# A hybrid attention, RWKV-7 and Hyena layer in fp32 on one core: the wkv output and its group norm with time on partitions, and two interleaved orders of small matrix products

## The chip, the cores and the metric

The kernel runs on one core of one Trainium2 chip. The metric is the device time of one execution in microseconds (us). The core has a matrix engine (TensorE, PE in the profile; PEld is its weight load), a vector engine (VectorE, DVE), a scalar engine (ScalarE, ACT), GpSimd (POOL) and a queue engine (SP) that issues most DMAs. A difference under about 0.2% (6 us) can't be told from no change here.

## What is computed

The reference is one step of a diffusion backbone with one layer. 128 context tokens and 256 latent tokens go through it together, so nearly every matrix product has 384 columns.

```python
h = rms_norm(x, ln1) * (1 + sc1) + sh1
proj = h @ w_in                       # attention q/k/v | wkv r/k/v | Hyena x0/x1/v | 3 gates
merged = g_a * (o_a @ w_pa) + g_r * (o_r @ w_pr) + g_c * (o_c @ w_pc)
x = x + ga1 * (merged @ w_out)
x = x + ga2 * (square(relu(h2 @ w_ff1 + b_ff1)) @ w_ff2 + b_ff2)
# the wkv mixer, 16 heads of 64, forward and backward in time, state S (value x key):
S = S * w_t + (S @ -kk_t) b_t^T + v_t k_t^T ;   y_t = S @ r_t
y = y_forward + flip(y_backward)
yn = (y - mean(y)) * rsqrt(var(y) + GN_EPS)     # per time step and head: the group norm
o_r = (yn * gn_g + gn_b + bonus) * g
```

## The kernel before

**Big products.** Each big product is made in tiles of 128 output features by 384 tokens. An fp32 weight block is split by ACT into a rounded part `whi` (L217) and by DVE into the rest `wlo` (L233), and each of the 16 blocks of 128 input features takes three matmuls (`hh·whi`, `hh·wlo`, `hl·whi`). They are the rows with `main` in the first part of the program, here called big matmuls.

**The mixers are side work.** While the big matmuls of the input projection run (about 235 to 1245 us in the profile), generators for the three mixers hand in small fp32 products between them: `rwkv(j)`, `hyena(j)`, `attention(j)`, for j = 0 to 7, each for two heads (128 features). After every third big matmul `side_step` advances each generator whose inputs should be there by a model of the three engines' clocks (`clk`), if DVE and ACT are not too far ahead of PE in that model. So the order on each engine is fixed when the program is built, by modelled costs, and each engine executes its list in order. Where a mixer of the next j needs a buffer of the last one, `drain` advances the generators alone, with no big matmuls between, until that mixer is done (in `a_done`, for instance, until attention j-1 is marked).

**The wkv mixer** works in 6 chunks of 64 time steps: two of the context (segment 0), four of the latents (segment 1), each in both directions d. First, 32x32 blocks of a triangular matrix are inverted on DVE and with small products: `quads` are the four blocks (two directions by two halves), each on its own 32 rows and columns of PE; `q1` is the first block of each direction in time (partitions 0 to 31 and 96 to 127). The products `g<-Z,Q` (48 for each j) and `g<-Q,Z` (24) go to two PSUM banks `g2[:, 0]` and `g2[:, 1]`. Then four stages `st` go along the chunks; a stage has two chunks (one for each direction) for each live segment, so 4, 4, 2 and 2. In each stage the output y of a chunk is made with features on partitions: one 128x128-weight product with the state (`misc<-kr,SZ`), and two with 64 weight columns (`misc<-Gm,UV`), one for each head. ACT copies them to `ys`.

**The tail** adds the directions, takes head means with a product by a block matrix (`misc<-ys,cst` 128x384), squares, sums them to time rows (`head_sums`, six products of 2 columns), takes the inverse root, turns that back (`spread`, three transposes), scales, and multiplies by the gate (`misc<-lg,l`).

**Attention** makes its output in three blocks of 128 queries; the two heads are in the two halves of the columns (`misc<-aPT,vt`), first all key tiles of head 0, then those of head 1.

Of the kernel before, what the change touches and what calls it, by code (L numbers as in the profile page):

```python
# [23 lines left out]
NT = NP + NS  # L24
# [110 lines left out]
def kernel(ctx: ExitStack, tc: tile.TileContext, t: dict, o: dict):  # L135
# [79 lines left out]
    def acopy(out, in_):  # L215
        spend("act", (free(in_) / 1.2 + 93) / 1000.0, out, (in_,))
        scalar.copy(out, in_)  # L217
# [20 lines left out]
    def add(out, a, b):  # L238
        tt(out, a, b, ALU.add)
# [15 lines left out]
    def turn(out, in_):  # L255
        dve(out, (in_,))
        vector.transpose(out, in_)  # L257
# [20 lines left out]
    def C(name):  # L278
        a, n = COFF[name]
        return cst[:, a:a + n]  # L280
# [425 lines left out]
    def open_a():  # L706
        p = pa.enter_context(tc.tile_pool(name="pa", bufs=1))

        def T(name, shape, dt=F32):
            P[name] = p.tile(shape, dt, name=name)  # L710
            return P[name]

        T("rkv", [128, 2, NT])
        T("v", [128, NT + 64])
        T("TW", [128, 2, NT]); T("TA", [128, 2, NT])
        T("cum", [128, NT]); T("tx", [128, NT])
        T("Pe", [128, 6, 65]); T("PC", [128, 2, 6])
        T("kk", [128, NT])
        for d in range(2):
            T(f"kr{d}", [128, 6, 2, 64]); T(f"bk{d}", [128, 6, 2, 64])  # L720
            T(f"UV{d}", [128, 6, 128]); T(f"Gm{d}", [128, 6, 2, 128])
        T("Z", [128, 32, 32]); T("L", [128, 32, 32]); T("Z2", [128, 32, 32])
        T("X", [128, 12, 64]); T("Q32", [128, 12, 32])
        T("SZ", [128, 2, 2, 128]); T("ys", [128, 2, NT])
        T("hy", [128, 3, NT]); T("qk", [128, NT]); T("kc", [128, 512]); T("va", [128, NT])
        P["pool"] = p
        flat = P["Z2"].rearrange("p i j -> p (i j)")
        P["QT"] = flat[:, :384].rearrange("p (b i) -> p b i", i=32)
        P["tmp"] = flat[:, 512:624]
        P["W0"] = P["L"].rearrange("p i j -> p (i j)")[:, 512:768].rearrange("p (a b) -> p a b", a=2)  # L730
        scalar.dma_start(out=T("dfi", [97, 1280]), in_=t["dfti"])
        nc.gpsimd.memset(P["Z"], 0.0)
        nc.gpsimd.memset(P["X"], 0.0)
        vcopy(P["Q32"], C("eye").unsqueeze(1).to_broadcast([128, 12, 32]))
# [34 lines left out]
    def take_g2():  # L769
        yield from take("g2")  # L770
# [4 lines left out]
    def take_m():  # L775
        i = yield from take(0, 1)
        return i
# [79 lines left out]
    def rwkv(j):  # L857
        rk_, v = P["rkv"], P["v"]
        r, k = rk_[:, 0], rk_[:, 1]
        TW, TA, cum, tx, Pe, PC = (P[n] for n in ("TW", "TA", "cum", "tx", "Pe", "PC"))  # L860
        kk = P["kk"]
        kr, bk, UV, Gm = ([P[f"{n}{d}"] for d in range(2)] for n in ("kr", "bk", "UV", "Gm"))
        Z, L, Z2, X, QT, tmp, W0, SZ, ys, Q32 = (P[n] for n in ("Z", "L", "Z2", "X", "QT", "tmp", "W0", "SZ", "ys", "Q32"))
        bon = P["pool"].tile([128, NT], F32, tag="bon", name="bon", bufs=2)
        l2 = P["pool"].tile([128, 3, 128], F32, tag="l2", name="l2", bufs=2)
        cj = slice(j * 128, j * 128 + 128)
# [79 lines left out]
                yield  # L946
        turn(Z, L.rearrange("p i j -> p j i"))
        turn(Z2, L)
        yield from take_g2()
        yield  # L950

# [9 lines left out]
                C("eye")[rows[d], x].unsqueeze(1).to_broadcast([64, 12, 16]), ALU.mult, ALU.add)  # L961
        yield
        for b in range(12):
            for d, q, s in quads:
                mm(g2[s, 0, b * 32:b * 32 + 32], Q32[s, b], DD[d][s, :, b])
        for b in range(12):
            for d in range(2):
                s = q1[d]
                mm(g2[s, 1, b * 32:b * 32 + 32], DD[d][s, :, b], Q32[s, b])
        yield  # L970
        for d, q, s in quads:
            (acopy if d else vcopy)(X[s, :, 32 * q:32 * q + 32], g2[s, 0, :NT].rearrange("p (b t) -> p b t", t=32))
# [23 lines left out]
        for st in range(4):  # L996
            live = [(sg, d, seqs[sg][d][st]) for sg in ((1, 0) if st < 2 else (1,)) for d in range(2)]
            for sg in ((1, 0) if st < 2 else (1,)):
                first = sg == 0 and st == 0
                if not first:  # L1000
                    for d in range(2):
                        mm(PQ[d][rows[d], sg * 128:sg * 128 + 128], kr[d][:, seqs[sg][d][st], 0], SZ[:, sg, d], stop=False)
                for h in range(2):
                    for d in range(2):
                        c = seqs[sg][d][st]
                        mm(PQ[d][rows[d], sg * 128 + 64 * h:sg * 128 + 64 * h + 64], Gm[d][rows[1 - d], c, h, 0:64],
                           UV[d][rows[1 - d], c, 64 * h:64 * h + 64], start=first, stop=first or h == 1)
            yield
            n = 256 if st < 2 else 128
            s0 = 0 if st < 2 else 128  # L1010
            acopy(W0[rows[0]].rearrange("p a b -> p (a b)")[:, s0:s0 + n], PQ[0][rows[0], s0:s0 + n])
            vcopy(W0[rows[1]].rearrange("p a b -> p (a b)")[:, s0:s0 + n], PQ[1][rows[1], s0:s0 + n])
            yield
            for sg in ((1, 0) if st < 2 else (1,)):
                for h in range(2):
                    for d in range(2):
                        c = seqs[sg][d][st]
                        mm(PQ[1 - d][rows[d], sg * 128 + 64 * h:sg * 128 + 64 * h + 64], X[rows[d], 2 * c + h],
                           W0[rows[d], sg, 64 * h:64 * h + 64])
            yield  # L1020
            for sg, d, c in live:
                cpy = acopy if d == 0 else vcopy
                cpy(UV[d][rows[d], c], PQ[1 - d][rows[d], sg * 128:sg * 128 + 128])
            yield
            for sg, d, c in live:
                if sg == 1 and st == 3:
                    continue
                mm(PQ[d][:, 256 + sg * 128:384 + sg * 128], bk[d][:, c].rearrange("p a x -> p (a x)"), UV[d][:, c])
            m = yield from take_m()
            for n, (sg, d, c) in enumerate(live):  # L1030
                y = M[m][:, n * 64:n * 64 + 64]
                first = sg == 0 and st == 0
                if not first:
                    mm(y, SZ[:, sg, d], kr[d][:, c, 1], stop=False)
                for h in range(2):
                    mm(y[64 * h:64 * h + 64], UV[d][:, c, 64 * h:64 * h + 64], Gm[d][:, c, h, 64:128],
                       start=first, stop=True)
            yield
            for sg, d, c in live:
                if sg == 1 and st == 3:  # L1040
                    continue
                ps, S = PQ[d][:, 256 + sg * 128:384 + sg * 128], SZ[:, sg, d]
                if sg == 0 and st == 0:
                    stt(S, ps, PC[:, d, c:c + 1], C("bones"), ALU.mult, ALU.mult)
                else:
                    add(S, ps, S)
                    stt(S, S, PC[:, d, c:c + 1], C("bones"), ALU.mult, ALU.mult)
            for n, (sg, d, c) in enumerate(live):
                acopy(ys[:, d, c * 64:c * 64 + 64], M[m][:, n * 64:n * 64 + 64])
            give(m)  # L1050
            if st == 1:
                for d in range(2):
                    pool_q.dma_start(out=o["state"][d, j], in_=SZ[:, 0, d])
            if st == 3:
                mark("chain", j)
            yield
        y, yc2 = ys[:, 0], ys[:, 1]
        add(y, ys[:, 0], ys[:, 1])
        m = yield from take_m()
        yield  # L1060
        mm(M[m][:, :NT], C("bones"), y)
        yield
        stt(y, M[m][:, :NT], -1.0 / 64, y, ALU.mult, ALU.add)
        dep()
        act(yc2, y, AF.Square)
        yield
        head_sums(M[m], yc2)
        yield
        rs = rsqrt(M[m][:, 0:6], 6, 1.0 / 64, 64e-5)
        dep()  # L1070
        acopy(ch(yc2), rs.unsqueeze(2).to_broadcast([128, 6, 64]))
        yield
        spread(M[m], yc2)
        yield
        mul(y, y, M[m][:, :NT])
        dep()
        act(y, y, AF.Identity, bias=V("gn_b", j), scale=V("gn_g", j))
        yield
        mm(M[m][:, :NT], l2[:, 2], P["lg"])
        yield  # L1080
        add(y, y, bon)
        mul(y, y, M[m][:, :NT])
        give(m)
        pool_q.dma_start(out=Osp[1, cj], in_=y)
        mark("tail", j)

# [55 lines left out]
    def attention(j):  # L1142
# [31 lines left out]
        for blk in range(3):  # L1174
# [42 lines left out]
            yield  # L1217
            m = yield from take_m()
            kts = (0,) if blk == 0 else (1, 2, 3)
            for h in range(2):  # L1220
                for i, kt in enumerate(kts):
                    mm(M[m][64 * h:64 * h + 64, 0:128], vt[:, kt, 64 * h:64 * h + 64], PT[:, h, i],
                       start=(i == 0), stop=(i == nk - 1))
            yield
# [473 lines left out]
```

## Time and profile before

| | |
|---|---|
| median of 3 runs | 2991.66 us (2987.81 to 2993.28) |
| the profiled execution | 2992.65 us, its span 2990.9 us |
| PE busy | 2937.0 us (98%), 20845 matmuls |
| DVE busy | 1864.9 us (62%) |
| ACT busy | 1226.1 us (41%) |
| DMA | 452.02 MB, mean 151 GB/s |

A matmul's busy time is modelled and overlaps its neighbours, so a sum of busy times is not the time that PE gave to something. The time that a group of small products takes is read from starts: from the start of the first to the start of the next big matmul. An fp32 product that is no transpose shows as two rows (x2); a big matmul and a transpose show as one. The start of one big matmul follows another's by 0.17 us.

### The profile page before, as it was taken

The page shows a single profiled execution, that of the slowest core. Times are in us where ns is not written, and L with a number is a line of the kernel's source. Part 1 is how long each engine was busy: PE and PEld are TensorE (multiplying, and loading weights), DVE is VectorE, ACT ScalarE, POOL GpSimd, SP SyncE. Part 2 cuts the span into 40 slices and gives each one's busy share as a digit, 9 for nine tenths or more (in the row PEclk, how much of TensorE's full clock was granted, in tenths as well). Part 3 has the DMA queues.
Part 4 walks back from the last instruction along what each step waited for, and adds up shares of the span by engine and source line. Part 5 has one row for each costly group of instructions (what it writes and reads, how often), then busy time and mean ns, then how long its engine had stood idle before and what let it go on. Part 6 is the DMA issues. An engine that isn't in the chain of part 4 may idle for free.

```text
span 2990.9 us, 52326 instructions
## 1 busy us (share of the span) xinstructions
PE 2937.0 (98%) x20845; PEld 2752.4 (92%) x20845; DVE 1864.9 (62%) x3777; ACT 1226.1 (41%) x2523; POOL 121.1 (4%) x213
## 2 busy tenths in 40 slices
PE   6999999999999999999999999999999999999997
PEld 2598989888898989899999999999999999999997
DVE  4266757666675767488888889758444444444444
ACT  3353544545354444423333334443344234324443
POOL 0001101100101110000000000000000000000000
PEclk8999999999999999999999999999999999999998
DMA  9933333333333333487776777557444444444443
GB/s 330 327 108 99 103 88 113 96 92 97 99 102 96 104 91 109 130 283 215 223 223 202 227 223 228 170 162 215 127 124 130 127 118 122 134 126 121 127 127 106
DMA packets 682664, 452.02 MB, mean 151 GB/s; under 512 B 19220, under 2 KB 626405, under 8 KB 682418
## 3 DMA queue, kind: packets, MB, share of 16 engines
q1 hardware_dynamic: 627768, 347.63, 39.3%
q10 hardware_dynamic: 46330, 81.21, 8.4%
q0 software_dynamic: 8320, 19.83, 2.3%
q8 instruction: 163, 2.67, 0.4%
q14 instruction: 83, 0.68, 0.1%
HBM read 433.50 MB, written 15.10 MB: 150 GB/s over the span
## 4 chain that ended last, share of the span: by engine, by line
PE 90%; DVE 4%; issue 2%; DMA 1%; ACT 1%; POOL 0%; ACTq 0%; SPq 0%; DVEq 0%; POOLq 0%
PE main L198 49%; PE pq L198 31%; PE misc L198 5%; PE g L198 4%; PE misc L202 1%; DVE L L257 1%; DMA raw<-in_w_in_dram 1%; DVE macc L253 1%; DVE wlo L233 1%; DMA mraw<-in_w_mod_dram 0%; ACT whi L217 0%; ACT Z L217 0%; DMA ot<-Osp 0%; DVE hB L233 0%; DVE x L233 0%
## 5 line engine op out<-in xcount | busy, mean ns | idle before, releaser
L233 DVE TENSOR_TENSOR wlo<-raw,whi 128x512 fp32r<-128x512 f32 x1164 | 776.6, 686 | 472.3 <-ACT whi L217 471.6
L217 ACT CAST whi<-raw 128x512 fp32r<-128x512 f32 x1164 | 690.7, 618 | 453.7 <-PE main L198 198.4
L198 PE MATMUL main<-hh,whi 128*128 128x384 f32 (+1 forms) x2128 | 757.6, 356 | 4.8 <-ACT whi L217 4.7
L198 PE MATMUL main<-hl,whi 128*128 128x384 f32 (+1 forms) x2128 | 719.6, 338 | 0.0
L198 PE MATMUL main<-hh,wlo 128*128 128x384 f32 (+1 forms) x2128 | 719.1, 338 | 0.5 <-DVE wlo L233 0.4
L198 PEld LDWEIGHTS main<-hh,whi 128*128 128x128 f32 x2128 | 402.7, 189 | 40.5 <-issue 22.7
L198 PEld LDWEIGHTS main<-hh,wlo 128*128 128x128 f32 x2128 | 403.5, 190 | 6.6 <-issue 2.6
L198 PEld LDWEIGHTS main<-hl,whi 128*128 128x128 f32 x2128 | 402.8, 189 | 2.4 <-DVE wlo L233 0.8
L253 DVE SCALAR_TENSOR_TENSOR macc<-mw,cvec,macc 128x512 f32<-128x512 f32 x480 | 337.4, 743 | 0.6 <-DMA mw<-in_w_mod_dram 0.6
L198 PE MATMUL pq<-hh,whi 128*128 128x386 f32 (+1 forms) x816 | 276.1, 338 | 0.0
L198 PE MATMUL pq<-hh,wlo 128*128 128x386 f32 (+1 forms) x816 | 275.2, 337 | 0.1
L198 PE MATMUL pq<-hl,whi 128*128 128x386 f32 (+1 forms) x816 | 275.0, 337 | 0.0
L198 PE MATMUL main<-mh,whi 128*128 128x384 f32 x640 | 214.2, 335 | 0.0
L198 PE MATMUL pq<-mh,whi 128*128 128x384 f32 x640 | 213.9, 334 | 0.0
L198 PE MATMUL main<-ml,whi 128*128 128x384 f32 x640 | 213.9, 334 | 0.0
L198 PE MATMUL main<-mh,wlo 128*128 128x384 f32 x640 | 213.8, 334 | 0.0
L198 PE MATMUL pq<-mh,wlo 128*128 128x384 f32 x640 | 213.8, 334 | 0.0
L198 PE MATMUL pq<-ml,whi 128*128 128x384 f32 x640 | 213.8, 334 | 0.0
L213 ACT ACTIVATE rl<-rl,bb 128x128 f32<-128x128 f32 (+1 forms) x128 | 51.4, 448 | 281.0 <-DVE rl L233 281.0
L198 PEld LDWEIGHTS pq<-hh,whi 128*128 128x128 f32 x816 | 153.5, 188 | 2.0 <-issue 1.9
L198 PEld LDWEIGHTS pq<-hh,wlo 128*128 128x128 f32 x816 | 153.5, 188 | 0.9 <-DVE wlo L233 0.7
L198 PEld LDWEIGHTS pq<-hl,whi 128*128 128x128 f32 x816 | 153.5, 188 | 0.0
(341 smaller groups left out, 3806.9 us busy)
## 6 DMA issues: line engine op xcount, KB each, us to landing
raw<-in_w_ff_dram SPq DMA_DIRECT2D x256, 512.0 KB, 3.9
raw<-in_w_in_dram SPq DMA_DIRECT2D x234, 512.0 KB, 3.8
mw<-in_w_mod_dram ACTq DMA_DIRECT2D x256, 256.0 KB, 3.5
mraw<-in_w_mod_dram SPq DMA_DIRECT2D x32, 1024.0 KB, 8.5
raw<-in_w_out_dram SPq DMA_DIRECT2D x32, 512.0 KB, 4.5
raw<-in_w_pc_dram SPq DMA_DIRECT2D x16, 512.0 KB, 4.2
raw<-in_w_pa_dram SPq DMA_DIRECT2D x16, 512.0 KB, 6.1
raw<-in_w_pr_dram SPq DMA_DIRECT2D x16, 512.0 KB, 4.2
```

The costliest lines, as they stand in the source:

```text
L198: tensor.matmul(out, lhsT=lhsT, rhs=rhs, start=start, stop=stop)
L202: tensor.transpose(out, in_, ident)
L213: scalar.activation(out, in_, func, **kw)
L217: scalar.copy(out, in_)
L233: vector.tensor_tensor(out, a, b, op)
L253: vector.scalar_tensor_tensor(out, a, s, b, op0, op1)
L257: vector.transpose(out, in_)
```

## The change

It has three parts. (1) In the wkv stages the operands of the y products change places: `kr` and `Gm` become the weights (64 columns, time) and `SZ` and `UV` stream, so y lies with time on partitions, 64 rows for each direction of the stage. The two directions write the two column halves in turn. The first direction that reaches a chunk is copied by ACT, the second is added by DVE. The group norm is then two DVE reductions along the free axis; three transposes bring the result back to features on partitions, in the same step as the gate product, into the `PQ` banks. (2) The 32x32 products: the four blocks go in the order 0, 3, 1, 2; the 24 products of the second kind take their weights from a packed copy `DC` (12 columns of 32, made by ACT and DVE before) and stand between those of the first kind. (3) Attention's output products alternate between the heads.

```diff
-        T("SZ", [128, 2, 2, 128]); T("ys", [128, 2, NT])
+        T("SZ", [128, 2, 2, 128]); T("ys", [128, 2, NT]); T("gs", [128, 2, 6]); T("DC", [128, 12, 32])
...
+        for d in range(2):
+            (acopy if d else vcopy)(DC[q1[d]], (Z, Z2)[d][q1[d]][:, :, :12].rearrange("p i b -> p b i"))
         yield from take_g2()
...
         for b in range(12):
-            for d, q, s in quads:
+            for i in (0, 3, 1, 2):
+                d, q, s = quads[i]
                 mm(g2[s, 0, b * 32:b * 32 + 32], Q32[s, b], DD[d][s, :, b])
-        for b in range(12):
-            for d in range(2):
-                s = q1[d]
-                mm(g2[s, 1, b * 32:b * 32 + 32], DD[d][s, :, b], Q32[s, b])
+                if b % 2 == 1 and i % 3:
+                    for d in range(2):
+                        mm(g2[q1[d], 1, (b + i - 2) * 32:(b + i - 1) * 32], DC[q1[d], b + i - 2], Q32[q1[d], b + i - 2])
...
-            for n, (sg, d, c) in enumerate(live):
-                y = M[m][:, n * 64:n * 64 + 64]
+            for sg in ((1, 0) if st < 2 else (1,)):
                 first = sg == 0 and st == 0
+                here = [(d, seqs[sg][d][st], M[m][rows[seqs[sg][d][st] % 2], sg * 128:sg * 128 + 128]) for d in range(2)]
                 if not first:
-                    mm(y, SZ[:, sg, d], kr[d][:, c, 1], stop=False)
+                    for d, c, y in here:
+                        mm(y, kr[d][:, c, 1], SZ[:, sg, d], stop=False)
                 for h in range(2):
-                    mm(y[64 * h:64 * h + 64], UV[d][:, c, 64 * h:64 * h + 64], Gm[d][:, c, h, 64:128],
-                       start=first, stop=True)
+                    for d, c, y in here:
+                        mm(y[:, 64 * h:64 * h + 64], Gm[d][:, c, h, 64:128], UV[d][:, c, 64 * h:64 * h + 64],
+                           start=first, stop=first or h == 1)
...
-            for n, (sg, d, c) in enumerate(live):
-                acopy(ys[:, d, c * 64:c * 64 + 64], M[m][:, n * 64:n * 64 + 64])
+            for sg, d, c in live:
+                y, x = yt[rows[c % 2], c // 2], M[m][rows[c % 2], sg * 128:sg * 128 + 128]
+                if st < (1, 2)[sg]:
+                    acopy(y, x)
+                else:
+                    add(y, x, y)
...
-        add(y, ys[:, 0], ys[:, 1])
-        m = yield from take_m()
-        yield
-        mm(M[m][:, :NT], C("bones"), y)
-        yield
-        stt(y, M[m][:, :NT], -1.0 / 64, y, ALU.mult, ALU.add)
...
-        head_sums(M[m], yc2)
...
-        spread(M[m], yc2)
...
+        vector.tensor_reduce(s1, y6, mybir.AxisListType.X, ALU.add)
+        stt(y6, s1.unsqueeze(2).to_broadcast([128, 6, 64]), -1.0 / 64, y6, ALU.mult, ALU.add)
         dep()
+        act(ys[:, 1], ys[:, 0], AF.Square)
+        yield
+        dve(q6, (q6,))
+        vector.tensor_reduce(s2, q6, mybir.AxisListType.X, ALU.add)
+        rs = rsqrt(s2, 6, 1.0 / 64, 64e-5)
+        mul(y6, y6, rs.unsqueeze(2).to_broadcast([128, 6, 64]))
+        yield
+        for i in range(3):
+            transp(PQ[0][:, i * 128:(i + 1) * 128], yt[:, i])
+        mm(PQ[1][:, :NT], l2[:, 2], P["lg"])
...
-            for h in range(2):
-                for i, kt in enumerate(kts):
+            for i, kt in enumerate(kts):
+                for h in range(2):
                     mm(M[m][64 * h:64 * h + 64, 0:128], vt[:, kt, 64 * h:64 * h + 64], PT[:, h, i],
```

On PE, the y products of the second stage stood like this before (`kr_1059`, `Gm_1062` and `UV_1061` belong to the forward direction, `kr_1063`, `Gm_1066` and `UV_1065` to the backward one; `64x64` and `128x64` are output rows by columns):

```order
L198 MATMUL misc_72<-kr_1059,SZ 128x64
L198 MATMUL misc_72<-Gm_1062,UV_1061 64x64 x2
L198 MATMUL misc_72<-kr_1063,SZ 128x64
L198 MATMUL misc_72<-Gm_1066,UV_1065 64x64 x2
L198 MATMUL misc_72<-kr_1059,SZ 128x64
L198 MATMUL misc_72<-Gm_1062,UV_1061 64x64 x2
L198 MATMUL misc_72<-kr_1063,SZ 128x64
L198 MATMUL misc_72<-Gm_1066,UV_1065 64x64 x2
```

The full-width product with `kr` stood in front of each pair of half-width ones, four times. The same stage on PE now:

```order
L198 MATMUL misc_72<-SZ,kr_1059 64x128
L198 MATMUL misc_72<-SZ,kr_1063 64x128
L198 MATMUL misc_72<-UV_1061,Gm_1062 64x64
L198 MATMUL misc_72<-UV_1065,Gm_1066 64x64
L198 MATMUL misc_72<-UV_1061,Gm_1062 64x64
L198 MATMUL misc_72<-UV_1065,Gm_1066 64x64
L198 MATMUL misc_72<-SZ,kr_1059 64x128
L198 MATMUL misc_72<-SZ,kr_1063 64x128
L198 MATMUL misc_72<-UV_1061,Gm_1062 64x64
L198 MATMUL misc_72<-UV_1065,Gm_1066 64x64
L198 MATMUL misc_72<-UV_1061,Gm_1062 64x64
L198 MATMUL misc_72<-UV_1065,Gm_1066 64x64
```

All 12 are half-width, the directions take turns, and no full-width product stands among them.

On PE, the start of the 32x32 products now (`Z` and `Z_1069` are the two directions' inverses, `Q_1071` the factor `Q32`); before, all 48 of the first kind stood ahead of the 24 of the second:

```order
L198 MATMUL g_71<-Z,Q_1071 32x32
L198 MATMUL g_71<-Z_1069,Q_1071 32x32
L198 MATMUL g_71<-Z,Q_1071 32x32
L198 MATMUL g_71<-Z_1069,Q_1071 32x32
L198 MATMUL g_71<-Z,Q_1071 32x32
L198 MATMUL g_71<-Z_1069,Q_1071 32x32
L198 MATMUL g_71<-Z,Q_1071 32x32
L198 MATMUL g_71<-Q_1071,DC 32x32 x2
L198 MATMUL g_71<-Z_1069,Q_1071 32x32
L198 MATMUL g_71<-Q_1071,DC 32x32 x2
```

Two pairs of the second kind stand in each group of twelve.

On PE, where `rwkv(3)` makes its Gram blocks (`g<-kr,bk`) and big matmuls of j = 3 end, before:

```order
L198 MATMUL g_71<-kr_1063,bk_1064 128x128 x8
L198 MATMUL misc_72<-zt,dff 97x128 x8
L198 MATMUL main_69<-hh,whi 128x384
L198 MATMUL main_69<-hh,wlo 128x384
L198 MATMUL main_69<-hl,whi 128x384
L202 MATMUL misc_73<-cst,bk_1060 128x128 x4
L198 MATMUL main_69<-hh,whi 128x384
L198 MATMUL main_69<-hh,wlo 128x384
L198 MATMUL main_69<-hl,whi 128x384
L198 MATMUL g_71<-kr_1063,bk_1064 128x128 x4
L198 MATMUL misc_72<-zt,dff 97x128 x2
```

Big matmuls lay between the Gram products, and attention j = 2 had ended earlier. The same place on PE now:

```order
L198 MATMUL main_69<-hl,whi 128x384
L198 MATMUL g_71<-kr_1059,bk_1060 128x128 x8
L202 MATMUL misc_72<-cst,v 128x128 x2
L198 MATMUL g_71<-kr_1059,bk_1060 128x128 x4
L202 MATMUL misc_72<-cst,aS 128x128 x3
L202 MATMUL misc_73<-cst,aS 128x128 x3
L198 MATMUL g_71<-kr_1063,bk_1064 128x128 x8
L202 MATMUL misc_72<-cst,bk_1060 128x128 x4
L198 MATMUL misc_73<-aPT,vt 64x128 x6
L202 MATMUL misc_72<-cst,bk_1060 128x128 x2
L198 MATMUL g_71<-kr_1063,bk_1064 128x128 x4
L198 MATMUL main_70<-hh,whi 128x384
```

The end of attention j = 2 (`aS`, `aPT`) and the Gram blocks of j = 3 now stand in one run with no big matmul in it; it is a `drain` of `a_done`, and the only one of this kind in the order.

## Rows read from the trace of the kernel before

**Rows 1.** The page: busy time by engine, and the chain that ended last
```profile
PE 2937.0 (98%) x20845; PEld 2752.4 (92%) x20845; DVE 1864.9 (62%) x3777; ACT 1226.1 (41%) x2523; POOL 121.1 (4%) x213
...
PE 90%; DVE 4%; issue 2%; DMA 1%; ACT 1%; POOL 0%; ACTq 0%; SPq 0%; DVEq 0%; POOLq 0%
```

**Rows 2.** Windows: length, busy (count) of PE, PEld, DVE, ACT, POOL; clock; DMA
```profile
235.00:1245.00 1010.00, 1003.13 (x9468) 898.78 (x9468) 674.80 (x1589) 468.31 (x1104) 112.29 (x195) 0.99 0.34 99
...
511.00:514.40 3.40, 3.40 (x11) 3.40 (x12) 1.64 (x3) 1.52 (x4) 0.00 (x0) 0.50 0.04 11
```

**Rows 3.** Waits of PE, 235 to 1245 us: total us, times, longest
```profile
PE g L198 <- issue: 4.9, 6, 1.8
```

**Rows 4.** Timeline of PE, y products, j = 2: start, us, what, rows
```profile
528.51 0.33 PE L198 MATMUL misc<-kr,SZ 128*128 128x64 f32 x2
...
529.90 0.45 PE L198 MATMUL main<-hh,whi 128*128 128x384 f32 x1
...
541.36 0.33 PE L198 MATMUL misc<-kr,SZ 128*128 128x64 f32 x2
...
543.78 0.45 PE L198 MATMUL main<-hh,whi 128*128 128x384 f32 x1
...
556.49 0.33 PE L198 MATMUL misc<-kr,SZ 128*128 128x64 f32 x2
...
557.64 0.92 PE L198 MATMUL g<-kc,qk 64*128 64x384 f32 x4
```

**Rows 5.** Timeline of PE: runs whose products alternate between column halves
```profile
524.55 0.34 PE L198 MATMUL main<-hl,whi 128*128 128x384 f32 x1
524.81 0.68 PE L198 MATMUL pq<-L,X 64*64 64x64 f32 x16
525.43 0.45 PE L198 MATMUL main<-hh,whi 128*128 128x384 f32 x1
...
562.25 0.45 PE L198 MATMUL pq<-L,X 64*64 64x64 f32 x8
...
534.99 0.44 PE L198 MATMUL misc<-aPT,vt 128*64 128x128 f32 x4
535.36 0.44 PE L198 MATMUL main<-hh,whi 128*128 128x384 f32 x1
```

**Rows 6.** Timeline of PE: attention output, second block of queries
```profile
553.81 1.15 PE L198 MATMUL misc<-aPT,vt 128*64 128x128 f32 x12
554.89 0.44 PE L198 MATMUL main<-hh,whi 128*128 128x384 f32 x1
```

**Rows 7.** Timeline of PE: group norm, head means and head sums
```profile
569.39 0.81 PE L198 MATMUL misc<-ys,cst 128*128 128x384 f32 x2
570.13 1.14 PE L198 MATMUL misc<-aPT,vt 128*64 128x128 f32 x12
...
573.49 0.52 PE L198 MATMUL misc<-cst,ys 128*64 128x2 f32 x12
573.86 0.50 PE L198 MATMUL misc<-cst,tx 128*64 128x2 f32 x12
```

**Rows 8.** Timeline of PE: 32x32 products; in brackets idle time and its releaser
```profile
507.01 1.55 PE L198 MATMUL g<-Z,Q 32*32 32x32 f32 x96
508.37 0.75 PE L198 MATMUL g<-Q,Z 32*32 32x32 f32 x21
510.02 0.98 PE L198 MATMUL g<-Q,Z 32*32 32x32 f32 x27 [0.89 <-issue]
510.93 0.67 PE L198 MATMUL main<-hh,whi 128*128 128x384 f32 x1
...
515.82 0.95 PE L198 MATMUL g<-L,Gm 32*32 32x32 f32 x48
```

**Rows 9.** Groups by line, 235 to 1245 us, DVE: busy us, mean ns, idle
```profile
L233 DVE TENSOR_TENSOR Gm<-g,cst 128x1024 f32<-128x1024 f32 x14 | 17.1, 1220 | 2.2 <-PE g L198 2.2
...
L253 DVE SCALAR_TENSOR_TENSOR kr<-kk,Pe 128x384 f32<-128x384 f32 x14 | 7.7, 550 | 0.0
```

More of the change, by code (lines that the diff above doesn't have):

```diff
@@ L860, in rwkv @@
         TW, TA, cum, tx, Pe, PC = (P[n] for n in ("TW", "TA", "cum", "tx", "Pe", "PC"))
-        kk = P["kk"]
+        kk, DC = P["kk"], P["DC"]
         kr, bk, UV, Gm = ([P[f"{n}{d}"] for d in range(2)] for n in ("kr", "bk", "UV", "Gm"))
         Z, L, Z2, X, QT, tmp, W0, SZ, ys, Q32 = (P[n] for n in ("Z", "L", "Z2", "X", "QT", "tmp", "W0", "SZ", "ys", "Q32"))
+        yt = by128(ys[:, 0])
         bon = P["pool"].tile([128, NT], F32, tag="bon", name="bon", bufs=2)
@@ L948, in rwkv @@
         turn(Z2, L)
+        on()
+        yield
+        for d in range(2):
+            (acopy if d else vcopy)(DC[q1[d]], (Z, Z2)[d][q1[d]][:, :, :12].rearrange("p i b -> p b i"))
         yield from take_g2()
@@ L1056, in rwkv @@
             yield
-        y, yc2 = ys[:, 0], ys[:, 1]
-        add(y, ys[:, 0], ys[:, 1])
-        m = yield from take_m()
+        y6, q6 = (ys[:, i].rearrange("p (g x) -> p g x", x=64) for i in range(2))
+        s1, s2 = P["gs"][:, 0], P["gs"][:, 1]
+        dve(y6, (y6,))
+        vector.tensor_reduce(s1, y6, mybir.AxisListType.X, ALU.add)
+        stt(y6, s1.unsqueeze(2).to_broadcast([128, 6, 64]), -1.0 / 64, y6, ALU.mult, ALU.add)
+        dep()
+        act(ys[:, 1], ys[:, 0], AF.Square)
         yield
-        mm(M[m][:, :NT], C("bones"), y)
+        dve(q6, (q6,))
+        vector.tensor_reduce(s2, q6, mybir.AxisListType.X, ALU.add)
+        rs = rsqrt(s2, 6, 1.0 / 64, 64e-5)
+        mul(y6, y6, rs.unsqueeze(2).to_broadcast([128, 6, 64]))
         yield
-        stt(y, M[m][:, :NT], -1.0 / 64, y, ALU.mult, ALU.add)
-        dep()
-        act(yc2, y, AF.Square)
-        yield
-        head_sums(M[m], yc2)
-        yield
[L1069 to L1072, printed above, removed]
-        spread(M[m], yc2)
[L1074 to L1080, printed above, removed]
+        for i in range(3):
+            transp(PQ[0][:, i * 128:(i + 1) * 128], yt[:, i])
+        mm(PQ[1][:, :NT], l2[:, 2], P["lg"])
+        yield
+        y = ys[:, 1]
+        act(y, PQ[0][:, :NT], AF.Identity, bias=V("gn_b", j), scale=V("gn_g", j))
+        dep()
         add(y, y, bon)
-        mul(y, y, M[m][:, :NT])
-        give(m)
+        mul(y, y, PQ[1][:, :NT])
         pool_q.dma_start(out=Osp[1, cj], in_=y)
```

## The prediction

> **What bounds the kernel now.** I read the page first, then the stretch in which the change lies, then the starts of PE's instructions in one j. PE is busy for 98% of the span and the chain that ended last is 90% PE, DVE 4% [rows 1]. The reader is to see that no other engine comes near: in the input projection, 235 to 1245 us, PE is busy for 1003 of 1010 us, DVE for 675, ACT for 468 [rows 2]. What PE waits for there in front of the 32x32 products is 4.9 us in six places, by "issue", that is, for nothing that the profile shows [rows 3]. So PE's list in this stretch sets its length, and a side product costs what it takes from the row of big matmuls. All three parts of the change are side products in this stretch; after it nothing is changed. I cost each part by j = 2, from start to start, and multiply by 8.
>
> **The y products.** Before, the stages took 1.39 us (528.51 to 529.90), 2.42 (541.36 to 543.78) and 1.15 (556.49 to 557.64) [rows 4]; the fourth is like the third. Sum 6.11 us for each j. Each full-width product stands between half-width ones, and every change of width costs. Now each stage is one run of half-width products whose halves alternate. Their price comes from three runs that do so already [rows 5]: eight products of 64 columns from 524.81 to 525.43, 0.62 us; the durations of eight and of four such products, 0.68 and 0.45, differ by 0.23, so 0.058 each, and 0.62 - 8 x 0.058 = 0.156 for a run as such; two of 128 columns from 534.99 to 535.36, 0.37, so (0.37 - 0.156) / 2 = 0.107 each. The first stage has two of 128 and eight of 64: 0.83. The second four and eight: 1.05. The third and fourth two and four: 0.60 each. Together 3.08. The big matmul (or full-width state product) in front of a half-width run is longer: 524.55 to 524.81 is 0.26 instead of 0.17 [rows 5], 0.09 for each of four stages, 0.36. So 6.11 - 3.44 = 2.67 us for each j, **-21.4 us**. The bounds are in the first rival (-13.9) and at no cost of the four front switches (-24).
>
> ACT gives half of its y copies to DVE, which adds instead, and DVE gains two reductions and a few products of 384 columns while it loses three of that size. DVE has 335 us of slack in the stretch [rows 2], so I cost this at nothing; if it comes late in the wkv chain, that is the third rival.
>
> **Attention's output.** In the second and third block of queries the six products of 128 columns took 553.81 to 554.89, 1.08 us [rows 6]. In turn between the halves they take 6 x 0.107 + 0.156 = 0.80. 0.28 x 16 = **-4.5 us**. The first block has one key tile and stood alternately before. Bounds 0 (no overlap) and -5.
>
> **The group norm.** PE loses the head means, 569.39 to 570.13 or 0.74, of which 0.09 is the switch to the next run, so 0.65; and the head sums, 573.49 to 573.86, 0.37 [rows 7]. The three transposes stay, only of another tensor, and so does the gate product. 1.02 x 8 = **-8.2 us**. The tail has fewer returns between engines, and nothing waits for it but the next chain. Bounds -5 (if the steps that remain cost a switch more) and -9.
>
> **The 32x32 products.** 48 of the first kind took 507.01 to 508.37, 0.028 us each; the 24 of the second kind cost 0.51 us for the first ten and a half, then PE stood idle for 0.89 us for nothing that the profile shows, and 0.91 us for the rest [rows 8], about 0.057 each. What differs is that their weights are read with a stride. `g<-L,Gm`, 24 products with packed weights, has a duration of 0.95 in all [rows 8], its last instruction's own length included, so well under 0.04 each. With packed weights and other blocks between, I take 0.028 for all: 24 x 0.029 = 0.69 us, -5.5 us over 8 j. But the idle stretch lies inside this run, and I read it as instructions that are not there yet (an estimate: the page shows no other cause, and the six places all lie in these dense runs). Then its end is set by something that began earlier, and what the run saves ahead of it is waited for instead. The number of products is the same. I take half, **-3 us**; bounds 0 and, with four blocks at a time and no idle time, -19.
>
> The Trainium skill speaks against this part, in "TensorEngine Tiling (Array Packing)", "Gotcha 1: PSUM Pressure": different row tiles can't access one PSUM bank at the same time. By it the second kind was slow because both of its row tiles write bank 1, and packed weights help nothing; the term would be 0 and the sum 3 us less. But the first kind lets four row tiles write bank 0 at 0.028 us each, half of 0.057 [rows 8], so in this trace row tiles share a bank at no such price, and I keep the -3.
>
> **The run without big matmuls.** The order shows one drain that was not there: `a_done` for j = 3 finds attention j = 2 unfinished, and 24 Gram products, 14 transposes and six attention products follow each other with no big matmul between. There PE waits for DVE. From its first Gram products on DVE owes a `Gm` of 1.22 us, four products for `kr` and `bk` of 0.55, a second, smaller `Gm` (an estimate: about half, 0.7) and one more `Gm` of 1.22 ahead of the last four products [rows 9]: 5.3 us, and three returns over PE that I put at 1 us each, so 8 to 9 us. PE's own work in it, which it would do elsewhere, is about 24 x 0.107 + 0.80 + 14 x 0.11 = 4.9 us by the rates above. The difference is some **+4 us**; bounds 0 and +9 (nothing overlaps). After such idle time the clock may fall: from 511.0 to 514.4 us, right behind the idle 0.89 us, the granted clock was 0.50, the 1.2 GHz level [rows 2]; there are five such stretches in this part of the program, each behind 32x32 products. One costs 3.4 us at half speed, **+1.7 us**, and I leave the other five as they are.
>
> **Sum.** -21.4 - 4.5 - 8.2 - 3 + 4 + 1.7 = -31.4 us. Against the profiled execution's 2992.65 us that is 2961.2. The profiled execution lies 1.0 us above the median of the runs shown, so the forecast for a median is **2960 us**, 1.05% faster.
>
> **Rivals.**
> 1. *The alternating pairs overlap less in one bank.* The runs of rows 5 that I priced by write two banks (`pq`), save one; the y pairs write one. At the rate of the attention run that stays in one half for three products, (1.08 - 0.156) / 6 = 0.154 for 128 columns and half of it for 64 [rows 6], the stages take 1.08, 1.39, 0.77 and 0.77, with the switches 4.37; y gains 1.74 x 8 = 13.9, and attention nothing. Sum -31.4 + 7.5 + 4.5 = -19.4: 2972 us. For it: the one-bank pair in rows 5 is a short one. Against: it already costs 0.37, no more than two at 0.107. Chance 0.15.
> 2. *The dense runs lose their idle time and their half clock too.* If the blocks run four at a time (0.014 each, 72 products 1.0 us instead of 2.73, -13.8), the 4.9 us of idle time go [rows 3], and with them the five half-clock stretches (5 x 1.7 = 8.5 us), the sum is -21.4 - 4.5 - 8.2 - 13.8 - 4.9 - 8.5 + 5.7 = -55.6: 2936 us. Against it: the number of instructions in the run is unchanged, and a faster run leaves less time to bring them. Chance 0.08.
> 3. *Slower: PE waits in the chain of stages.* A stage goes PE, copy, PE, copy, PE, and DVE now has two or four adds in each of the 32 stages queued ahead of the next stage's copy. If PE's list reaches the next step before DVE does, each stage costs a wait. With 1.3 us in each it is 41.6 us against -31.4, +10: 3002 us; it decides from 1.2 us a stage. For it: in the drain above the planner shows that DVE's load now counts. Against: the state update stands ahead of the adds in DVE's list, the planner spaces steps by their costs, and before no wait of PE for DVE weighs in this stretch (1003 of 1010 us busy). Chance 0.04.
> 4. *The gain is eaten by several such waits or by a drain several times longer,* to within 0.2% (6 us, what a measurement can tell from no change): 0.05.
>
> **How the numbers follow.** The forecast's own case (2950 to 2969) holds 0.68. Faster by over 0.2%: 0.68 + 0.15 + 0.08 = 0.91; within 0.2%: 0.05; slower: 0.04. The range 2943 to 2976 takes in the first rival, the bounds of the drain and of the small products, and leaves out rivals 3 and 4 and most of rival 2.
>
> **What would show it.** In the new profile the three `y` groups should be half-width, `misc<-SZ,kr` and `misc<-UV,Gm`, the second stage of a j about 1.05 us from its first start to the next big matmul, and attention's six products 0.80. No `misc<-ys,cst` of 384 columns should be left, and the three transposes stand right ahead of the gate product. The drain should show as one idle stretch of PE, waiting for DVE `Gm`, near 640 us. The number of half-clock stretches in the projection should be five or six. The prediction is wrong if the second stage takes over 1.3 us, if PE's waits for DVE or ACT in the stretch sum to over 15 us, or if the idle time in the 32x32 products grows by more than they save.

## The result and the profile after

The changed kernel takes 2957.23 us (median of 4 runs, 2955.82 to 2957.55) against 2992.47 before (2987.81 to 2995.10): ratio 0.9883, 95% interval 0.9866 to 0.9900, 1.2% faster. The forecast was 2960 with a range of 2943 to 2976. The profiled execution took 2957.55 us, 35.1 less than before; the forecast sum was -31.4.

The page's first row and its chain, after, answer to [rows 1]:

```profile
PE 2893.9 (98%) x20733; PEld 2716.7 (92%) x20733; DVE 1883.1 (64%) x3841; ACT 1230.7 (42%) x2475; POOL 121.1 (4%) x213
PE 84%; DVE 8%; issue 3%; DMA 3%; ACT 2%; POOL 0%; ACTq 0%; SPq 0%; DVEq 0%; POOLq 0%
```

PE still sets the end, but the chain now holds 8% of DVE where it held 4%. The windows of the projection, now some 35 us shorter, and of the three stretches in it at the lower clock (length, then busy time and count of PE, PEld, DVE, ACT, POOL; clock; DMA) answer to [rows 2]:

```profile
235.00:1210.00 975.00, 961.52 (x9362) 865.11 (x9361) 693.14 (x1654) 473.21 (x1056) 112.67 (x196) 0.99 0.35 103
246.80:250.21 3.41, 3.41 (x19) 3.35 (x20) 1.64 (x3) 1.04 (x3) 0.00 (x0) 0.50 0.11 31
376.51:379.92 3.41, 3.41 (x12) 3.14 (x10) 1.44 (x3) 1.77 (x4) 0.00 (x0) 0.50 0.00 0
594.96:601.79 6.83, 6.54 (x42) 5.43 (x44) 3.99 (x8) 4.90 (x11) 0.00 (x0) 0.50 0.03 11
```

PE's idle share has doubled: 13.5 of 975 us, where it was 6.9 of 1010. Its waits from 235 to 1245 us (total us, times, longest) answer to [rows 3]:

```profile
PE g L198 <- ACT L L217: 4.3, 5, 1.1
PE g L198 <- DVE Gm L233: 3.5, 3, 2.8
PE g L198 <- issue: 2.8, 3, 1.4
PE g L198 <- DVE Q L253: 1.3, 3, 0.4
```

Less waiting by issue, but three waits for other engines that were not there. The second y stage of j = 2 on PE answers to [rows 4]:

```profile
535.87 0.44 PE L198 MATMUL misc<-SZ,kr 128*64 128x128 f32 x4
536.13 0.40 PE L198 MATMUL misc<-UV,Gm 128*64 128x64 f32 x8
536.37 0.39 PE L198 MATMUL misc<-SZ,kr 128*64 128x128 f32 x4
536.59 0.40 PE L198 MATMUL misc<-UV,Gm 128*64 128x64 f32 x8
536.92 0.45 PE L198 MATMUL main<-hh,whi 128*128 128x384 f32 x1
```

From 535.87 to 536.92 it is 1.05 us, the forecast number; before it was 2.42. Attention's six products in the second block of queries of j = 2:

```profile
566.29 0.88 PE L198 MATMUL misc<-aPT,vt 128*64 128x128 f32 x12
567.10 0.44 PE L198 MATMUL main<-hh,whi 128*128 128x384 f32 x1
```

They take 0.81 us, where 0.80 was forecast and 1.08 measured before [rows 6]. The 32x32 products of j = 2 now begin and end so, and `g<-L,Gm` comes behind them:

```profile
502.53 0.41 PE L198 MATMUL g<-Z,Q 32*32 32x32 f32 x16 [0.43 <-DVE Q L253]
504.75 0.44 PE L198 MATMUL main<-hh,whi 128*128 128x384 f32 x1
508.15 0.95 PE L198 MATMUL g<-L,Gm 32*32 32x32 f32 x48 [1.05 <-ACT L L217]
```

That is 2.22 us for 72. Before, two j showed no idle time in them (for j = 2 see [rows 8]); j = 1 took 3.13 us and j = 5 took 2.80:

```profile
905.32 1.55 PE L198 MATMUL g<-Z,Q 32*32 32x32 f32 x96
906.68 1.51 PE L198 MATMUL g<-Q,Z 32*32 32x32 f32 x48
908.12 0.44 PE L198 MATMUL main<-hh,whi 128*128 128x384 f32 x1
```

The run without big matmuls:

```profile
590.96 1.16 PE L198 MATMUL g<-kr,bk 64*128 64x128 f32 x16
592.05 0.44 PE L202 MATMUL misc<-cst,v 128*128 128x128 f32 x2
595.25 1.23 PE L198 MATMUL g<-kr,bk 64*128 64x128 f32 x8 [2.76 <-DVE Gm L233]
596.41 1.54 PE L202 MATMUL misc<-cst,aS 128*128 128x128 f32 x6
```

One idle stretch waiting for `Gm`, as forecast, with a double stretch at the lower clock on it (last row of the windows above).

Where the 35 us went is read by adding up, for each group, the times from one PE start to the next between the same two big matmuls of both programs (237 to 1351 us before, 237 to 1317 after, 1114.4 and 1079.1 us); idle time and the excess at the lower clock are taken out and stand for themselves.

| term | forecast, us | measured, us |
|---|---|---|
| y products | -21.4 | -24.3 in the stages, +0.7 and +2.3 for the switch in front of them (2.3 in `pq<-UV,bk`): -21.2 |
| attention's output | -4.5 | -4.3, +0.8 in front: -3.5 |
| group norm | -8.2 | -8.5 |
| 32x32 products | -3 | -5.8 in the products, -2.1 in idle time by issue: -7.9 |
| the run without big matmuls | +4 | 2.8 idle, 2.7 more for transposes: +5.5 |
| lower clock | +1.7 | -3.1 |
| waits for `L`, `Q`, `UV`, `Gm`, less those for `hB` | none | +5.5 |
| width changes at other insertions (312 before, 278 after) | none | -3.4 |
| other idle time, most of it behind the projection | none | +2.2 |
| rest | none | -0.9 |
| sum | -31.4 | -35.3 |

### The profile page after: what moved, and what is told of

It reads as the page before. It is cut to its first block, busy times and chain, and to the rows that moved or that the text cites. A ratio compares the mean times of both kernels' runs of the same rounds, so it can differ in the third digit from the quotient of the medians.

```text
span 2955.4 us, 52128 instructions
## 1 busy us (share of the span) xinstructions
PE 2893.9 (98%) x20733; PEld 2716.7 (92%) x20733; DVE 1883.1 (64%) x3841; ACT 1230.7 (42%) x2475; POOL 121.1 (4%) x213
## 4 chain that ended last, share of the span: by engine, by line
PE 84%; DVE 8%; issue 3%; DMA 3%; ACT 2%; POOL 0%; ACTq 0%; SPq 0%; DVEq 0%; POOLq 0%
PE main L198 44%; PE pq L198 31%; PE misc L198 4%; PE g L198 4%; DVE wlo L233 2%; DVE macc L253 1%; PE misc L202 1%; DMA raw<-in_w_in_dram 1%; DMA raw<-in_w_pc_dram 1%; DVE L L257 1%; ACT whi L217 1%; DVE Z L257 0%; DVE Z L233 0%; DMA mraw<-in_w_mod_dram 0%; DVE L L233 0%
```

## The experiments

Medians of the runs stand against the kernel before on the same chip; "groups" are sums from start to start as in the table.

**y_by_direction.** One direction's y products after the other's.

```diff
-                if not first:
-                    for d, c, y in here:
+                for d, c, y in here:
+                    if not first:
                         mm(y, kr[d][:, c, 1], SZ[:, sg, d], stop=False)
-                for h in range(2):
-                    for d, c, y in here:
+                    for h in range(2):
```

> The changed kernel with one thing put back: in a stage the y products of one direction stand together (state product, then both heads), then those of the other, instead of in turn between the column halves. Operands, shapes, number of products and the order of everything else stay. Theory 1 (two products overlap only where they lie in different column halves): at 0.154 us for 128 columns and 0.077 for 64 instead of 0.107 and 0.058 the y products of the projection take 38.6 us instead of 24.7, and the time is 2957 + 14 = 2971 us. Rival (what counted was that no full-width product stands between them any more; the halves' turn is worth nothing): 24.7 us stay, 2957 us.

Measured 2964.67 us, ratio 0.9906 [0.9891, 0.9920]; the y group 34.1 us instead of 24.7. The expectation's sum was wrong: the rates that it names give 32.1, so +7.4; 13.9 is what the rival leaves of the gain. The second stage, from its first start to the next big matmul:

```profile
534.46 0.43 PE L198 MATMUL misc<-SZ,kr 128*64 128x128 f32 x2
535.88 0.44 PE L198 MATMUL main<-hh,whi 128*128 128x384 f32 x1
```

It took 1.42 us (1.39 by those rates). So the halves' turn is worth 9.4 us of the 24.3 that the y products gain, and the rest comes with the half width, no full-width product standing among them.

**kinds_apart, strided_weights.** The old order with the packed weights, and the new order with the strided ones (`DD[d][q1[d], :, b + i - 2]` in place of `DC[q1[d], b + i - 2]`).

```diff
-            for i in (0, 3, 1, 2):
-                d, q, s = quads[i]
+            for d, q, s in quads:
                 mm(g2[s, 0, b * 32:b * 32 + 32], Q32[s, b], DD[d][s, :, b])
-                if b % 2 == 1 and i % 3:
-...
+        for b in range(12):
+            for d in range(2):
+                s = q1[d]
+                mm(g2[s, 1, b * 32:b * 32 + 32], DC[s, b], Q32[s, b])
```

> The changed kernel with the order of before in the 32x32 products: all 48 of the first kind (blocks 0, 1, 2, 3), then all 24 of the second, still with the packed weights DC. Theory 1 (the strided read of the weights made the second kind slow, packing alone mends it): 72 products at 0.028 are 2.0 us for each j without idle time, now 2.22, so -1 to -2 us over eight j: 2956 us. Rival (the interleaving mends it): the 24 stay at 0.057, 2.73 us for each j, +4 us: 2961 us. The idle stretches stay where the 256-instruction blocks of PE's list end, whatever the order in the run.

> The changed kernel, but the 24 products of the second kind read their weights from Z and Z2 with the stride again instead of from DC (the copies to DC are still made, so the order of all work stays). Theory 1 (the strided weight read is the price): 24 x 0.029 = 0.7 us more for each j, 2.9 instead of 2.22, +5.5 us: 2963 us. Rival (interleaved among the first kind the slow weight loads are hidden behind other row tiles): 2.22 us for each j stay, 2957 us.

Measured 2956.46 us, 0.9879 [0.9862, 0.9895], and 2959.84 us, 0.9888 [0.9873, 0.9903]. Neither time can be told from the 2957 of the changed kernel; the groups can. The 32x32 group over eight j, without idle time:

| | kinds apart | interleaved |
|---|---|---|
| strided weights | 24.1 us (before) | 21.1 us |
| packed weights | 18.8 us | 18.3 us (after) |

Packing is nearly all of the gain; the order adds 0.5 us to it and hides half of the strided load where there is one. In kinds_apart, j = 3:

```profile
635.47 1.54 PE L198 MATMUL g<-Z,Q 32*32 32x32 f32 x96
636.82 0.95 PE L198 MATMUL g<-Q,DC 32*32 32x32 f32 x48
637.70 0.44 PE L198 MATMUL main<-hh,whi 128*128 128x384 f32 x1
```

24 products of the second kind take 0.88 us, 0.037 each, with the switch back to big matmuls in it; before they took 1.44 us in j = 5, 0.060 each. By the Trainium skill's rule that was weighed ("TensorEngine Tiling (Array Packing)", "Gotcha 1: PSUM Pressure") packing could not have helped, since both row tiles still write one bank; this trace disagrees.

**heads_in_sequence.** Attention's two loops exchanged back.

> The changed kernel with attention's output products head after head again. Theory 1 (products that stay in one column half don't overlap): aPT products 1.08 instead of 0.8 us for each of 16 blocks, their group in the projection goes from 15.9 us back to about 20, +3.5 to +4.5 us: 2961 us. Rival (the order of halves doesn't matter): the group stays at 15.9, 2957 us.

Measured 2961.27 us, 0.9894 [0.9879, 0.9908], 4 us more than the changed kernel, which alone would not be told from it. Its group took 20.1 us instead of 15.9, and the block shown above 1.07 instead of 0.81: theory 1, +4.3.

```profile
566.52 1.14 PE L198 MATMUL misc<-aPT,vt 128*64 128x128 f32 x12
567.59 0.44 PE L198 MATMUL main<-hh,whi 128*128 128x384 f32 x1
```

**no_norm_part, no_32x32_part.** The change without its y and norm part, and without its 32x32 part.

> The kernel before with the 32x32 part and attention's alternation, without the y products and the group norm of the change. In the order on PE only 12 big matmuls (j = 0 to 2) or 6 (j = 3 to 7) now stand between the 32x32 products and the products that read L, where before stood 18. Theory 1 (the four copies X, X, L, L behind the 32x32 products run one after the other on VectorE and ScalarE, 3.2 us, so 12 big matmuls leave a wait of about 1.0 us and 6 leave 2.1): PE waits 3 x 1.0 + 5 x 2.1 = 13 us for L, which eats the -3.5 of attention and the -5.5 of the 32x32 products, and the two parts alone make the kernel no faster: 2992 - 9 + 13 = 2996 us. Rival (those waits arise from the new y stages, not from the order): no such waits, 2992 - 9 = 2983 us.

Measured 3000.58 us (2998.22 to 3004.71), ratio 1.0034 [1.0022, 1.0046]: two of the three parts alone make the kernel slower, though their groups save 9.7 us. Its waits of PE, and j = 5:

```profile
PE g L198 <- ACT L L217: 12.1, 8, 1.9
PE g L198 <- DVE Q L253: 2.2, 5, 0.5
```

```profile
916.59 0.95 PE L198 MATMUL g<-L,Gm 32*32 32x32 f32 x48 [1.91 <-ACT L L217]
```

Theory 1 said 13; the lower clock cost 4.7 us more than before besides.

> The changed kernel without the 32x32 part (order and strided weights of before, no copies to DC), with y, group norm and attention as changed. Its order has no run without big matmuls near j = 3; 12 big matmuls stand ahead of the products that read L in seven j, 18 in one. Theory 1 (the drain, 2.8 us of idle time and 2.7 us more for its transposes, comes with the step that the 32x32 part adds, and its cost goes with it): +5.6 for the products, -5.5 for the drain, +2 for the waits for L (7 x 0.9 instead of 4.3), so 2959 us, within what can be told from 2957. Rival (the work of the drain waits as long elsewhere): 2957 + 5.6 + 2 = 2965 us.

Measured 2969.01 us (2964.77 to 2972.08), 0.9923 [0.9908, 0.9938]. The 2.8 us stretch is gone, but theory 1 fails on the time: PE now waits seven times for each of two other tiles, and side work is put between big matmuls 308 times instead of 278.

```profile
PE g L198 <- DVE Z L257: 4.4, 7, 0.6
PE g L198 <- ACT L L217: 4.2, 4, 1.0
PE g L198 <- issue: 4.0, 6, 1.5
PE g L198 <- DVE Gm L233: 2.5, 7, 0.4
```

**l_first.** The two copies to `L` ahead of those to `X`. First the copies in the changed kernel, on DVE and on ACT:

```profile
504.87 1.11 DVE L221 COPY X<-g 32x384 f32<-32x384 f32 x2 [1.66 <-PE g L198]
507.05 0.55 DVE L221 COPY L<-g 32x384 f32<-32x384 f32 x1 [1.07 <-ACT X L217]
```

```profile
506.06 0.95 ACT L217 COPY X<-g 32x384 f32<-32x384 f32 x2 [4.55 <-DVE X L221]
507.63 0.47 ACT L217 COPY L<-g 32x384 f32<-32x384 f32 x1 [0.61 <-DVE L L221]
```

They run one after the other, 504.87 to 508.10; the planner's costs put the two engines side by side.

> The changed kernel with one swap: behind the 32x32 products the two copies to L are issued ahead of the four to X. The order on PE is the same. Theory 1 (the copies run one after the other, and the products that read L wait for the last): L is ready some 1.1 us behind the products instead of 3.2, 12 big matmuls cover it, the 4.3 us of waits in front of g<-L,Gm go: 2953 us. Rival (X is now late, and the wait moves to the products that read X): 4.3 us in front of g<-X,Z, 2957 us.

Measured 2954.81 us (2951.68 to 2959.45), not to be told from 2957. Both theories fail: the wait stays at the same products and only changes its releaser, since half of them write, by the kernel's code, to the bank that the copies to `X` read.

```profile
PE g L198 <- ACT X L217: 4.1, 4, 1.1
```

**ahead_3_5, copies_costed, copies_costed_3.** Changes to the planner alone: DVE's allowed lead; a line `cur["t"] += 0.9` behind the copies; that line with a lead of 3.0.

> The changed kernel with one number of the planner changed: a side step may be taken while the modelled VectorE is up to 3.5 us ahead of the modelled PE, not 2.5. The order has no drain near j = 3. Theory 1 (the drain costs its 2.8 us of idle time, 2.7 us of transposes outside their cover and the half clock behind it): no idle stretch near 595 us, 2957 - 5.5 - 3.4 = 2948 us. Rival (VectorE's load comes late elsewhere): as many us of waits for VectorE in front of smaller groups, 2955 to 2959 us.

> The changed kernel with one line more in the planner: behind the copies to X and L the generator's ready time is 0.9 us later, the time by which the copies in a row (3.2 us) outlast the model's two engines side by side. In the order 18 big matmuls then stand ahead of the products that read L in every j, and the drain near j = 3 is gone. Theory 1 (the waits for L and the drain are faults of the planner's costs, not of the change): -4.3 for the waits, -2.8 for the drain's idle time, -2.7 for its transposes, -1.7 for its half clock, +2 for 35 more insertions, so 2957 - 9.5 = 2948 us. Rival (18 big matmuls only move the wait to another place of the chain, as the two copies to L put first did): 2955 to 2957 us, with as much waiting for VectorE and ScalarE elsewhere.

> The same line, and VectorE may be 3.0 us ahead of PE in the model, not 2.5. 18 big matmuls or more ahead of the products that read L, no drain, and 25 fewer insertions of side work between big matmuls than in the run with the line alone. Theory 1 (what an insertion costs, some 0.15 us from the changes of width in front of it and behind it, counts besides): 4 us less than that run, 2944 us. Rival (VectorE being further ahead makes waits for it that eat this): the same as the line alone or slower.

Measured 2955.20 (2954.26 to 2960.00), 2955.02 (2953.71 to 2955.45) and 2952.60 us (2948.48 to 2956.13). All three orders lose the drain, and the last two lose the waits for `L` (4.3 us to 0.1 and 0), yet only 2 to 5 us of some 10 arrive, less than the 6 that can be told. In ahead_3_5 idle time by issue in the 32x32 products grew from 2.8 to 8.4 us. The waits of copies_costed:

```profile
PE g L198 <- issue: 3.2, 2, 2.5
PE g L198 <- DVE Q L253: 2.8, 7, 0.4
PE g L198 <- DVE Gm L233: 2.5, 7, 0.4
```

Small waits for `Q` and `Gm` came back in seven j, and 35 more insertions cost 2.4 us behind them.

**no_norm_costed.** The parts without y and norm, with the line and a lead of 2.0.

> The kernel before with the 32x32 part and attention's alternation, as in the run without the y and group norm part, but with the planner's line for the copies (0.9 us) and VectorE at most 2.0 us ahead, which gives an order with 18 big matmuls ahead of the products that read L in every j and no drain. Theory 1 (these two parts are worth what their products save, and in the other order it was eaten by 12.1 us of waits for L and 4.7 us of half clock): -4.3 + 0.8 for attention and -5.6 + 0.3 for the 32x32 products against before, 2992 - 9 = 2983 us. Rival (part of the saving is lost in waits in any order): 2990 us or more.

Measured 2977.33 us (2973.93 to 2980.11), 0.9953 [0.9941, 0.9966], where theory 1 said 2983; no wait for `L`, and against before the lower clock costs 6.4 us less. The same two parts are worth +9 us in one order and -14 in another.

**shifted.** copies_costed_3 with 26 small products in front:

```diff
+        if i == 0:
+            for _ in range(26):
+                tensor.matmul(PQ[1][:64, :32], lhsT=f1, rhs=zp[:, :32], start=True, stop=True)
```

> The kernel with the line for the copies and VectorE 3.0 us ahead (copies_costed_3), and 26 small products (64x32, their result is not used) put into PE's idle time at 4 us, so that everything behind them stands 104 instructions later in PE's list; the order is otherwise the same. In all runs so far an idle stretch by issue in the 32x32 products stands at instruction 193 or 194 of a block of 256, and none where that lies less than 86 instructions behind the start of these products. The shift puts it at 34 to 88 instead of 138 to 192 in j = 1, 3, 5 and 7, and at 171 to 207 instead of 19 to 55 (and 275) in j = 0, 2, 4 and 6. Theory 1 (PE waits for instructions that have not been brought yet, by the place in the list): no idle time by issue in j = 1, 3 and 5 (now 1.43, 0.79, 0.86 us), 0 to 1.5 us each in the even j at the new places; the sum falls from 7.4 to some 3 us, 2949 us. Rival (the idle time belongs to the place in the program, to what the queues bring at that time): the same j keep the same idle time, 7.4 us, 2953 us.

Measured 2951.12 us (2949.88 to 2952.55), 0.9863 [0.9847, 0.9880]. The idle time moved with the list. j = 1 in copies_costed_3, then j = 2 in shifted:

```profile
372.84 0.22 PE L198 MATMUL g<-Q,DC 32*32 32x32 f32 x2 [1.43 <-issue]
374.07 0.59 PE L198 MATMUL main<-hh,whi 128*128 128x384 f32 x1
```

```profile
502.95 0.21 PE L198 MATMUL g<-Z,Q 32*32 32x32 f32 x1 [0.47 <-issue]
503.91 0.44 PE L198 MATMUL main<-hh,whi 128*128 128x384 f32 x1
```

In shifted j = 1, 3 and 5 have none and run through in 2.22 us; j = 0, 2, 4, 6 and 7 have 2.32, 0.47, 1.21, 0.95 and 0.69, 5.6 in all. One more stretch by issue, 1.48 us, stands in the big matmuls right behind the products of j = 1, and a double stretch at the lower clock begins in it (its row as in the windows above):

```profile
375.74 0.69 PE L198 MATMUL main<-hh,wlo 128*128 128x384 f32 x1 [1.48 <-issue]
```

```profile
375.07:381.90 6.83, 6.16 (x33) 5.72 (x35) 1.48 (x3) 3.02 (x6) 0.48 (x1) 0.50 0.01 2
```

Theory 1 holds for the place, and the sum was guessed too low (some 3). Of all kernels run this is the fastest, 6 us under the changed kernel and just about what can be told from it; against the kernel before it is clear.

## Why the prediction was right

**y, attention, group norm.** Right by their own steps: -33.2 measured where -34.1 was said. The group norm's share is read from the starts alone; no run takes it out by itself. That the first rival had its price about right (1.42 for the second stage, 1.39 said) and not its condition is shown by y_by_direction: the turn between the halves makes the overlap, in one bank too.

**32x32 products.** Mis-sized: -3 was said, -7.9 measured. The step that failed is "what the run saves ahead of it is waited for instead". The estimate behind it, that the idle time is instructions that are not there yet, is borne out: every one of the 69 idle stretches of PE by issue between 235 and 1245 us, over 14 profiles, stands at instruction 192 to 194 of a block of 256 of PE's list and ends 1.2 to 1.6 us after a packet of the instruction queue has ended (counted over weight loads, matmuls and waits; the queue brought 162 packets for the 20733 matmuls and as many weight loads of the changed kernel, one for some 256), and shifted moves them. But a run can meet one only where the block ends in it, and not every run that could meet one does, so the faster run lost two thirds of its saving to it in one order (ahead_3_5) and none in another.

**The run without big matmuls.** The place in the order and the tile waited for held, at 595 us where "near 640" was said. That the size is close (+5.5 for +4) is in part luck: the idle time was 2.8, and the other 2.7 are transposes that cost more with no big matmuls between, which the prediction put at nothing.

**The clock.** Wrong: +1.7 was said and five or six stretches in the projection, -3.1 and three came, the one behind the drain of double length; 1.7 of the -3.1 is a stretch behind the projection, at 1268.74 us before, that is gone. The step that failed is "I leave the other five as they are". They stood behind idle stretches by issue of 0.45 to 1.76 us; of the four such stretches that came (0.98, 1.41, 0.40 and 0.60 us) two have the lower clock behind them. All 42 stretches at 0.50 that the 14 profiles have from 235 to 1245 us stand just behind idle time of PE, of 0.4 to 2.8 us, or begin in it. But not all idle time is followed by one: the waits of 1.05 us in front of `g<-L,Gm` had none behind them, and in shifted none follows the 1.21 us of j = 4. Of the 23 idle stretches of 1.5 us and more, 20 have one. What else decides is open.

**What was missed.** Waits of +5.5 us in the chain behind the 32x32 products. The third rival looked for waits in the stages, where only 0.5 us came (`UV`). The order showed this one: 18 big matmuls (3.1 us) stood ahead of `g<-L,Gm` before, 12 (2.1 us) now in seven of eight j, and the copies take 3.2. The hidden gains at 34 fewer insertions (-3.4) and the clock covered the miss in the sum. So the total was nearer than its terms, and that is luck.

## What to carry to other kernels

Where a planner fixes the order by modelled costs, count what stands between a product and its reader before and after in the order, and hold it against the real length of the copies between them: a part that saves PE time can bring a wait that is larger than the saving, and the same edit is worth +9 or -14 us by the order alone. Small products on half of the columns should take turns between the halves even in one bank, and weights read with a stride are worth a packed copy (3 to 5 us here for 192 products).

## What was not expected of the hardware

Idle time by issue in dense runs of small products stands at one place in the instruction list. Of the 69 such stretches 58 are in front of 32x32 products and 11 in front of one of the big matmuls right behind them, and in 14 profiles none stood where the block of 256 ended less than 86 instructions behind the start of the products. At the same place the five kernels of one order agreed (0.9 to 1.6 us at 137, 0.4 to 0.7 at 178, none at 189). The place alone does not decide: shifted had 1.21 us at 189, and copies_costed none at 125, 141, 157 and 173, near which other orders had up to 1.9. Adding instructions elsewhere in the program moves it.
